# The first feed-forward's output of inner tiles 4 to 15 by seven block products, its modulation rows on GpSimd and ScalarE, and a shorter first look ahead in the second feed-forward

## The chip, the cores and the metric

The kernel runs on one core of a Trainium2 chip. The metric is the device time of one execution in microseconds; lower is better. The time before is the median of three runs.

## What is computed

One layer of a hybrid decoder block, for a sequence of 512 tokens with 1024 features, in float32:

```python
mod = silu(c) @ w_ada + b_ada              # nine rows of 1024: shift, scale, gate for three sub-layers
u = modulate(rmsnorm(h, g1), sh1, sc1)
h = h + 0.5 * gt1 * swiglu(u, w_ffn1_in, w_ffn1_out)
u = modulate(rmsnorm(h, g2), sh2, sc2)
h = h + gt2 * token_mixing(u, ...)         # pooling and dilated attention, gated
u = modulate(rmsnorm(h, g3), sh3, sc3)
h = h + 0.5 * gt3 * swiglu(u, w_ffn2_in, w_ffn2_out)
return rmsnorm(h, g_final)

def swiglu(u, w_in, w_out):
    a, b = split(u @ w_in, 2)              # 1024 -> 2 x 2816
    return (silu(a) * b) @ w_out           # 2816 -> 1024
```

The change touches the two `swiglu` and the computation of `mod`.

## The kernel before

All activations lie transposed, features on partitions, 512 tokens along the free dimension. Each float32 operand is split into a high part (`whi`, `HI`, `UH`) and a remainder (`wlo`, `HK`, `UL`), and each product is three matmuls: high by high, high by low, low by high. ScalarE (ACT) makes the high part with a copy (L312), VectorE (DVE) the low part with a subtraction (L326).

**Tiles and parts.** The 2816 inner features are 22 tiles of 128. `PARTS` groups them as 0 to 3, 4 to 7, 8 to 11, 12 to 15 and 16 to 21. `ffn` walks through the parts: it computes the hidden tiles of a part and one further pair, and then multiplies the hidden tiles of the part by the output weights and adds the result, times the gate, to the residual `H`.

**Two ways to compute hidden tiles.** `ffn_pair` (the first 8 tiles of the first feed-forward, the first 4 of the second) uses plain products, 512 tokens wide. `duo` computes a pair of tiles by seven block products (Strassen's scheme in Winograd's form): the contraction and the tokens are halved, the weights' sums are made on DVE (`make`, L251), the sums of the input once (`u_steps`), and the partial results are moved between PSUM banks and SBUF by ACT (`copy`, L746) and combined by DVE (L788, L807). Each block product is 24 matmuls of 256 tokens (L739 to L741).

**Two ways to compute an output.** The first feed-forward uses the plain one in all parts: 96 matmuls of 512 tokens (L357 to L359), an addition to `H` per output tile (L985). The second uses `out_quad` in its first four parts: seven block products of 24 matmuls with 256 tokens each (L865 to L867), with the hidden tiles' sums from `h_sums`, evictions by ACT (L848), combinations and additions by DVE (L895, L878, L871).

**Order of the weights.** `plan` writes the order in which weights are used. `look(n)` fetches by SyncE's DMA queue and splits weights up to n products ahead into a ring of seven products. For some products of the second feed-forward (`outer`) the low part is made by an ACT copy with scale -1 (L308) and a DMA of GpSimd's queue that accumulates the weights onto it (L310), instead of by DVE. `later(n, f)` puts off a step by n products; `todo` is a list of small steps, popped in the output's loops, such as the trigonometric tables (`trig`) in the third part's output of the first feed-forward.

**Modulation rows.** Each of the 72 columns of `mod` is a row product of 1024 elements, which `ada_do` computes on DVE with one multiplication and its accumulator (L380), from weights fetched by `ada_fetch` (L372). `bg` does one row at a time beside the first feed-forward, with the two buffers `cs` and `AR` from the end of the first part on: twice in each plain pair, and eight times in each plain output of the second to fourth parts, until 48 rows are done.

The engines' instruction order is the order in which this program emits them; each engine works through its own in order.

Of the kernel before, what the change touches and what calls it, by code (L numbers as in the profile page):

```python
# [14 lines left out]
P = 128  # L15
# [3 lines left out]
KT = 8  # L19
# [36 lines left out]
def lay_ffn(w_in, w_out, first, plain, blocks):  # L56

    ins, outs = [], []  # L60
    if first:
        cols = np.concatenate([c for j in range(first) for c in _tiles(j * P, DFF + j * P)])
        for k in range(KT):
            ins.append(w_in[k * P:(k + 1) * P][:, cols])
    for j in range(first, plain):
        for c in _tiles(j * P, DFF + j * P):
            ins.append(_fmajor(w_in, c))
    for j in range(plain, FT, 2):
        for i, c in ((0, 0), (0, DFF), (1, DFF), (1, 0)):
# [12 lines left out]
    outs = [np.concatenate(outs[i:i + 2], axis=1) for i in range(0, n, 2)] + outs[n:]  # L82
    return ins, quads + outs
# [44 lines left out]
NH = 6  # L128
# [15 lines left out]
class Kernel:  # L144
# [6 lines left out]
    def plan(self):  # L151
# [247 lines left out]
    def bg(self):  # L399
# [261 lines left out]
    def ffn_post(self, j, s, pb):  # L661
        nc = self.nc
        h = self.kept[j // 2 % 3][:, j % 2 * T:j % 2 * T + T] if self.kept else self.fw.tile([P, T], F32, name=("hf", "u3")[j % 2])
        nc.vector.tensor_tensor(h, s, pb, op=OP.mult)
        hh, hl = self.HH[j % NH], self.HL[j % NH]
        nc.scalar.activation(hh, h, AF.Copy)
        nc.vector.tensor_tensor(hl, h, hh, op=OP.subtract)

    def ffn_silu(self, j, pa):
        s = self.fw.tile([P, T], F32, name="sl" if j % 2 == 0 else "u2" if not self.kept else "p5")  # L670
        self.nc.scalar.activation(s, pa, AF.Silu)
        return s
# [70 lines left out]
    def duo(self, j, first, last):  # L743
# [15 lines left out]
        p5 = r(self.fw.tile([P, T], F32, name="p5"))  # L759
        if self.kept:  # L760
            c = self.kept[j // 2 % 3]
            u = q(self.fw.tile([P, 2 * T], F32, name="u2"))
            u2, u3 = u[:, :, 0, :], u[:, :, 1, :]
        else:
            c = self.fw.tile([P, 2 * T], F32, name="hf")
            u2, u3 = (r(self.fw.tile([P, T], F32, name=x)) for x in ("u2", "u3"))

        ts = slice(0, 1 if self.kept and j % 4 == 0 and j < PARTS[-1][0] else 2)
# [5 lines left out]
        def high():  # L774
            x = slice(j % NH * T, (j % NH + 2) * T)
            copy(q(self.HHall[:, x])[:, :, ts, :], q(c)[:, :, ts, :])

        def low():
            x = slice(j % NH * T, (j % NH + 2) * T)
            v.tensor_tensor(q(self.HLall[:, x])[:, :, ts, :], q(c)[:, :, ts, :], q(self.HHall[:, x])[:, :, ts, :],  # L780
                            op=OP.subtract)


        for i, (bank, u, start) in enumerate(((A, blk(lo4, T1), True), (B, S[0], True), (A, S[1], False),
                                              (C, blk(hi4, T1), False), (A, S[2], False), (B, S[3], False),
                                              (A, blk(hi4, T2), False))):
            if i == 6:
                v.tensor_tensor(q(c)[:, :, 1, :], p5, u3, op=OP.add)  # L788
            self.look(4)
# [7 lines left out]
            elif i == 1:  # L797
                copy(p5, r(B))
            elif i == 2:
                copy(u2, r(A))  # L800
# [4 lines left out]
            elif i == 6:  # L805
                silu(1, A)
                v.tensor_tensor(q(c)[:, :, 0, :], r(B), u2, op=OP.add)  # L807
# [4 lines left out]
        else:  # L812
            self.later(1, mult)
            self.later(2, high)
            self.later(2, low)

    def h_sums(self, k0):
# [5 lines left out]
        x = slice(k0 % NH * T, (k0 % NH + 2) * T)  # L823
        r = lambda x: x.rearrange("p (j t) -> p j t", j=2)
        to = [(r(h), r(l)) for h, l in self.G] + [(half(self.HHall[:, x], 1), half(self.HLall[:, x], 1))]
# [18 lines left out]
    def out_quad(self, k0, gate):  # L844
# [5 lines left out]
        blk = lambda k, t: [(self.HH[i % NH][:, t], self.HL[i % NH][:, t]) for i in (k, k + 1)]  # L850
# [5 lines left out]
        D = [self.fw.tile([P, 2 * T], F32, name=n).rearrange("p (j h t) -> p j h t", j=2, h=2) for n in ("u2", "sl")]  # L856
        p5 = [r(self.fw.tile([P, T], F32, name=n)) for n in ("p5", "p6")]
# [15 lines left out]
        for i, (bank, u, start) in enumerate(((A, blk(k0, T1), True), (B, G[0], True), (A, G[1], False),  # L873
# [8 lines left out]
            for b in range(2):  # L882
# [11 lines left out]
                elif i == 5:  # L894
                    v.tensor_tensor(D[b][:, :, 0, :], r(B[b]), D[b][:, :, 0, :], op=OP.add)  # L895
        for m in range(4):
# [5 lines left out]
    def ffn2(self):  # L902
        self.put, self.now = [], 0
        self.kept = [self.cond, self.cs, self.AR]
        bk = [self.nb() for _ in range(4)]
        self.head(2, bk, AF.Silu)
        self.G = [(self.tp.tile([P, T], F32R, name="ut"), self.fw.tile([P, T], F32R, name=f"G{i}")) for i in range(3)]
# [11 lines left out]
    def open_ffn(self):  # L919
# [3 lines left out]
        self.HHall, self.HLall = (fp.tile([P, NH * T], F32R, name=x) for x in ("HI", "HK"))  # L923
        self.HH, self.HL = ([x[:, i * T:(i + 1) * T] for i in range(NH)] for x in (self.HHall, self.HLall))
# [17 lines left out]
    def ffn(self, n, j, last=None):  # L942
# [10 lines left out]
        for part, (k0, k1) in enumerate(PARTS):  # L953
            tail = part + 1 == len(PARTS)
            while j < pairs_before(n, part):
# [3 lines left out]
                else:  # L959
                    if self.kept and not tail and j == k1:  # L960
# [7 lines left out]
            hk = [(self.HH[k % NH], self.HL[k % NH]) for k in range(k0, k1)]  # L968
            if not tail and n:
                self.out_quad(k0, gate)  # L970
                continue
            if not tail:
                for m in range(0, KT, 2):
# [8 lines left out]
                    for i, b in enumerate(bs):  # L982
# [4 lines left out]
                        if n == 0 and part:  # L987
                            self.bg()
# [42 lines left out]
    def beside_out(self, part):  # L1031

        if part == 0:
# [5 lines left out]
            self.sums = self.open_sums()  # L1039
            self.todo, last = self.u_steps(0)  # L1040
            return last
        if part == len(PARTS) - 1:
            assert self.ada_next == 48 and not self.adat, self.ada_next
# [423 lines left out]
    def build(self):  # L1467
# [39 lines left out]
        with self.open_ffn():  # L1507
            self.ada_pool = ExitStack()
            self.adaw = self.ada_pool.enter_context(tc.tile_pool(name="f1a", bufs=4))
            self.put, self.now, self.kept = [], 0, None  # L1510
# [4 lines left out]
        with self.open_ffn() as self.f2:  # L1515
# [130 lines left out]
def lay_inputs(x, c, positions, w_ada, b_ada, g_norm_ffn1, w_ffn1_in, w_ffn1_out, g_norm_mix, w_in, w_pool,  # L1646
# [4 lines left out]
    f1i, f1o = lay_ffn(A(w_ffn1_in)[0], A(w_ffn1_out)[0], FIRST, PLAIN[0], False)  # L1651
    f2i, f2o = lay_ffn(A(w_ffn2_in)[0], A(w_ffn2_out)[0], 0, PLAIN[2], True)
# [33 lines left out]
```

## Time and profile before

| | |
|---|---|
| median of 3 runs | 1015.61 us (1015.21 to 1018.82) |
| the profiled execution's own time | 1012.59 us |
| its span | 1010.8 us |
| hidden tiles and outputs of the first feed-forward, from the first duo to the last part's output | 125.9 to 326.9 us |
| the same of the second | 710.4 to 965.8 us |

How the rows of the profile are read: PE is TensorE, PEld its weight loads, DVE VectorE, ACT ScalarE, POOL GpSimd, SP SyncE; a q behind the name is the engine's queue of DMA issues. A row of the view by time gives start, duration (us), engine, line of the kernel, operation, output and inputs with their shapes, a count if several of one kind are merged, and in brackets how long the engine had been idle and what released it. A row of the view by groups gives count, busy time in us, mean ns of one, and the idle time ahead of it. A row of the view by stretches gives its bounds, its length, each engine's busy time, the granted TensorE clock as a share of the full one, the DMA engines' share and GB/s.

### The profile page before, as it was taken

The page shows a single profiled execution, that of the slowest core. Times are in us where ns is not written, and L with a number is a line of the kernel's source. Part 1 is how long each engine was busy: PE and PEld are TensorE (multiplying, and loading weights), DVE is VectorE, ACT ScalarE, POOL GpSimd, SP SyncE. Part 2 cuts the span into 40 slices and gives each one's busy share as a digit, 9 for nine tenths or more (in the row PEclk, how much of TensorE's full clock was granted, in tenths as well). Part 3 has the DMA queues.
Part 4 walks back from the last instruction along what each step waited for, and adds up shares of the span by engine and source line. Part 5 has one row for each costly group of instructions (what it writes and reads, how often), then busy time and mean ns, then how long its engine had stood idle before and what let it go on. Part 6 is the DMA issues. An engine that isn't in the chain of part 4 may idle for free.

```text
span 1010.8 us, 16369 instructions
## 1 busy us (share of the span) xinstructions
PE 996.5 (99%) x6652; PEld 916.6 (91%) x6652; DVE 789.2 (78%) x1182; ACT 496.4 (49%) x754; POOL 47.2 (5%) x54
## 2 busy tenths in 40 slices
PE   8999999999999999999999999999899999999997
PEld 6888898989999899889988888898899999999996
DVE  7978879889786777879447777577998988989754
ACT  6443252625435552233414233463677768677652
POOL 0000000000000000006100000000011011011001
PEclk9999999999999999999999999999999999999998
DMA  8866455555533413122154774321466656756712
GB/s 337 275 217 237 134 201 188 172 165 180 163 110 111 150 40 102 62 84 84 32 182 163 271 260 132 98 74 63 146 147 171 184 147 152 202 128 163 183 32 84
DMA packets 46574, 152.24 MB, mean 151 GB/s; under 512 B 5281, under 2 KB 8609, under 8 KB 46498
## 3 DMA queue, kind: packets, MB, share of 16 engines
q1 hardware_dynamic: 42354, 137.95, 41.0%
q0 software_dynamic: 3456, 12.58, 7.4%
q8 instruction: 52, 0.85, 0.3%
q10 hardware_dynamic: 688, 0.66, 0.2%
q14 instruction: 24, 0.20, 0.1%
HBM read 148.40 MB, written 2.77 MB: 150 GB/s over the span
## 4 chain that ended last, share of the span: by engine, by line
PE 91%; DVE 6%; ACT 1%; issue 1%; DMA 0%; DVEq 0%; ACTq 0%
PE bank L357 14%; PE bank L358 14%; PE bank L359 14%; PE bank L739 10%; PE bank L741 10%; PE bank L740 10%; PE bank L867 3%; PE bank L866 3%; PE bank L865 3%; PE bank L1616 1%; PE bank L1618 1%; PE bank L1620 1%; PE bank L1212 1%; DVE wlo L326 1%; PE bank L1391 1%
## 5 line engine op out<-in xcount | busy, mean ns | idle before, releaser
L326 DVE TENSOR_TENSOR wlo<-raw,whi 128x1024 fp32r<-128x1024 f32 (+7 forms) x161 | 160.1, 1008 | 59.9 <-ACT whi L312 59.5
L312 ACT ACTIVATE whi<-raw 128x1024 fp32r<-128x1024 f32 (+7 forms) x174 | 151.7, 890 | 29.8 <-DVE raw L251 28.1
L357 PE MATMUL bank<-UH,whi 128*128 128x512 f32 (+1 forms) x432 | 158.1, 366 | 0.0
L358 PE MATMUL bank<-UL,whi 128*128 128x512 f32 (+1 forms) x432 | 154.0, 357 | 0.1
L359 PE MATMUL bank<-UH,wlo 128*128 128x512 f32 (+1 forms) x432 | 153.9, 356 | 0.0
L741 PE MATMUL bank<-UH,wlo 128*128 128x256 f32 x512 | 141.8, 277 | 0.0
L739 PE MATMUL bank<-UH,whi 128*128 128x256 f32 x512 | 141.8, 277 | 0.0
L740 PE MATMUL bank<-UL,whi 128*128 128x256 f32 x512 | 141.8, 277 | 0.0
L326 DVE TENSOR_TENSOR wlo<-X,whi 128x1024 fp32r<-128x1024 f32 (+4 forms) x98 | 108.0, 1108 | 27.5 <-ACT whi L312 27.2
L312 ACT ACTIVATE whi<-X 128x1024 fp32r<-128x1024 f32 (+4 forms) x109 | 104.7, 973 | 38.0 <-DVE X L251 37.1
L739 PE MATMUL bank<-SH,whi 128*128 128x256 f32 x384 | 108.0, 281 | 2.9 <-ACT bank L746 2.9
L740 PE MATMUL bank<-SL,whi 128*128 128x256 f32 x384 | 107.6, 280 | 0.0
L741 PE MATMUL bank<-SH,wlo 128*128 128x256 f32 x384 | 107.6, 280 | 0.0
L357 PE MATMUL bank<-HI,whi 128*128 128x512 f32 (+1 forms) x278 | 96.8, 348 | 0.0
L740 PEld LDWEIGHTS bank<-UL,whi 128*128 128x128 f32 x512 | 96.4, 188 | 0.2
L358 PE MATMUL bank<-HK,whi 128*128 128x512 f32 (+1 forms) x278 | 96.5, 347 | 0.0
L739 PEld LDWEIGHTS bank<-UH,whi 128*128 128x128 f32 x512 | 96.2, 188 | 0.2
L359 PE MATMUL bank<-HI,wlo 128*128 128x512 f32 (+1 forms) x278 | 96.4, 347 | 0.0
L741 PEld LDWEIGHTS bank<-UH,wlo 128*128 128x128 f32 x512 | 96.1, 188 | 0.0
L359 PEld LDWEIGHTS bank<-UH,wlo 128*128 128x128 f32 x432 | 81.1, 188 | 12.1
L358 PEld LDWEIGHTS bank<-UL,whi 128*128 128x128 f32 x432 | 81.2, 188 | 11.7 <-issue 0.5
L357 PEld LDWEIGHTS bank<-UH,whi 128*128 128x128 f32 x432 | 81.2, 188 | 11.3 <-issue 0.5
(300 smaller groups left out, 2107.4 us busy)
## 6 DMA issues: line engine op xcount, KB each, us to landing
ada<-wada SPq DMA_DIRECT2D x47, 512.0 KB, 5.0
raw<-wmix SPq DMA_DIRECT2D x44, 512.0 KB, 3.9
raw<-wf1i SPq DMA_DIRECT2D x34, 512.0 KB, 4.6
raw<-wf2i SPq DMA_DIRECT2D x31, 512.0 KB, 3.7
wlo<-wf2i POOLq DMA_DIRECT2D x16, 512.0 KB, 6.2
X<-wf2i SPq DMA_DIRECT2D x13, 512.0 KB, 3.7
cs<-wada SPq DMA_DIRECT2D x12, 512.0 KB, 3.6
AR<-wada SPq DMA_DIRECT2D x12, 512.0 KB, 4.2
```

The lines of the kernel that those rows point to most:

```text
L312: self.nc.scalar.activation(self.hi[:, y], r[:, x], AF.Copy)
L326: self.nc.vector.tensor_tensor(self.lo[:, y], r[:, x], self.hi[:, y], op=OP.subtract)
L357: M(ps, hi, uh, start=start, stop=False)
L358: M(ps, hi, ul, start=False, stop=False)
L359: M(ps, lo, uh, start=False, stop=stop)
L739: M(o, hi, uh, start=start and p == 0 and k == 0, stop=False, skip_group_check=True)
L740: M(o, hi, ul, start=False, stop=False, skip_group_check=True)
L741: M(o, lo, uh, start=False, stop=k == 3, skip_group_check=True)
L865: M(o, hi, uh, start=start and m % 2 == 0 and k == 0, stop=False, skip_group_check=True)
L866: M(o, hi, ul, start=False, stop=False, skip_group_check=True)
L867: M(o, lo, uh, start=False, stop=k == 1, skip_group_check=True)
L1212: M(o, pt[:, blk * P:blk * P + P], v, start=i == 0, stop=i == len(srcs) - 1)
```

## The change

In the first feed-forward, parts two to four use `out_quad` with `h_sums`, so their output weights are laid out in blocks and pass through `blocks` in `plan`. Its duos after the first use the accumulating transfer for two of seven low parts, as those of the second do, and so do its quads. The hidden tiles' high and low parts get four tiles' room instead of six (`nh`), so those of some pairs are put off behind the quad that still reads the old ones. Intermediate tiles (`p5`, `u2`, `hf`) give way to three `kept` tiles. The modulation rows that the plain outputs did on DVE are multiplied by GpSimd and summed by ScalarE's accumulator in `beside`, after the second, fourth and sixth product of each duo and quad; the rows in plain pairs stay on DVE. The trigonometric steps are popped one per quad product. In the second feed-forward, the first duo's first product looks 3 products ahead instead of 4.

```diff
@@ lay_ffn
-        if blocks and k1 < FT:
+        if blocks <= k0 and k1 < FT:
@@ plan
-                        blocks(ins[at:at + 4], n == 2 and j > PLAIN[n])
+                        blocks(ins[at:at + 4], j > PLAIN[n])
...
-                put = blocks if n and part < len(PARTS) - 1 else plain
+                put = blocks if (n or part) and part < len(PARTS) - 1 else plain
@@ bg
         self.ada_do(self.ada_next)
+        self.bg_next()
+
+    def bg_next(self):
         self.ada_next += 1
         self.bg_fetch()
...
+    def bg_end(self):
+
+        if self.pending is None:
+            return
+        j, t = self.pending
+        self.pending = None
+        self.nc.scalar.activation(t, t, AF.Copy, accum_out=self.mod[:, j:j + 1])
+        self.ada_free.append(t)
+        self.bg_next()
+
+    def beside(self, i):
+
+        if self.nh != 4 or i not in (1, 3, 5) or self.ada_next >= self.ada_stop:
+            return
+        self.bg_end()
+        if self.ada_next < self.ada_stop and self.ada_next in self.adat:
+            t = self.adat.pop(self.ada_next)
+            self.nc.gpsimd.tensor_tensor(t, t, self.cond, op=OP.mult)
+            self.pending = self.ada_next, t
@@ ffn_post
+        if self.nh == 4 and j in (4, 5):
+            t = slice(0, HT)
+            self.later(5, lambda: nc.scalar.activation(hh[:, t], h[:, t], AF.Copy))
+            self.later(5, lambda: nc.vector.tensor_tensor(hl[:, t], h[:, t], hh[:, t], op=OP.subtract))
+            return
@@ duo
-            self.look(4)
+            self.look(3 if self.nh != 4 and first and i == 0 else 4)
...
+            self.beside(i)
...
-            self.later(2, high)
-            self.later(2, low)
+            n = 8 if self.nh == 4 and j % 4 == 0 else 2
+            self.later(n, high)
+            self.later(n, low)
@@ out_quad
+            if self.nh == 4 and self.todo:
+                self.todo.pop(0)()
+            self.beside(i)
@@ ffn
-                    if self.kept and not tail and j == k1:
+                    if not tail and j == k1:
                         self.h_sums(k0)
...
-            if not tail and n:
+            if not tail and (n or part):
                 self.out_quad(k0, gate)
                 continue
...
-                        if n == 0 and part:
-                            self.bg()
@@ beside_out
+            self.open_G()
...
+            self.bg_end()
@@ build
-        with self.open_ffn():
+        with self.open_ffn(4):
...
-        with self.open_ffn() as self.f2:
+        with self.open_ffn(6) as self.f2:
@@ lay_inputs
-    f1i, f1o = lay_ffn(A(w_ffn1_in)[0], A(w_ffn1_out)[0], FIRST, PLAIN[0], False)
+    f1i, f1o = lay_ffn(A(w_ffn1_in)[0], A(w_ffn1_out)[0], FIRST, PLAIN[0], PARTS[1][0])
```

More of the change, by code (lines that the diff above doesn't have):

```diff
@@ L82, in lay_ffn @@
     outs = [np.concatenate(outs[i:i + 2], axis=1) for i in range(0, n, 2)] + outs[n:]
-    return ins, quads + outs
+    return ins, outs[:-KT] + quads + outs[-KT:]
 def qk_cols(base, g, second):
@@ L758, in duo @@
         r = lambda x: x.rearrange("p (j t) -> p j t", j=2)
[L759 to L768, printed above, removed]
+        u3 = r(self.fw.tile([P, T], F32, name="u3"))
+        c = self.kept[j // 2 % 3]
+        c0, c1 = q(c)[:, :, 0, :], q(c)[:, :, 1, :]
+        ts = slice(0, 1 if j % 4 == 0 and j < PARTS[-1][0] else 2)
+        HHp, HLp = (q(x) for x in self.hpair(j))
         silu = lambda h, bank: nc.scalar.activation(q(s)[:, :, h, :], r(bank), AF.Silu)
@@ L822, in h_sums @@
         h11, h21, h12, h22 = half(a, 0), half(a, 1), half(b, 0), half(b, 1)
-        x = slice(k0 % NH * T, (k0 % NH + 2) * T)
         r = lambda x: x.rearrange("p (j t) -> p j t", j=2)
-        to = [(r(h), r(l)) for h, l in self.G] + [(half(self.HHall[:, x], 1), half(self.HLall[:, x], 1))]
+        to = [(r(h), r(l)) for h, l in self.G] + [tuple(half(x, 1) for x in self.hpair(k0))]
         def add(o, x, y, op):
@@ L855, in out_quad @@
         r = lambda x: x.rearrange("p (j t) -> p j t", j=2)
-        D = [self.fw.tile([P, 2 * T], F32, name=n).rearrange("p (j h t) -> p j h t", j=2, h=2) for n in ("u2", "sl")]
-        p5 = [r(self.fw.tile([P, T], F32, name=n)) for n in ("p5", "p6")]
+        D = [self.kept[k // 2 % 3].rearrange("p (j h t) -> p j h t", j=2, h=2) for k in (k0, k0 + 2)]
+        p5 = self.fw.tile([P, 2 * T], F32, name="sl")
+        p5 = [r(p5[:, i * T:(i + 1) * T]) for i in range(2)]
         def product(banks, u, start):
@@ L967, in ffn @@
             nk = k1 - k0
-            hk = [(self.HH[k % NH], self.HL[k % NH]) for k in range(k0, k1)]
-            if not tail and n:
+            hk = [self.hh(k) for k in range(k0, k1)]
+            if not tail and (n or part):
                 self.out_quad(k0, gate)
@@ L1506, in build @@
         self.ada_free, self.ada_depth = None, 3
-        with self.open_ffn():
+        with self.open_ffn(4):
             self.ada_pool = ExitStack()
             self.adaw = self.ada_pool.enter_context(tc.tile_pool(name="f1a", bufs=4))
-            self.put, self.now, self.kept = [], 0, None
+            self.put, self.now = [], 0
             self.startup()
```

50 lines of the change are left out of this document (29 added, 21 removed).

## The prediction, made before the result was known

> **What bounds the kernel now.** I read the page first, then the busy time of each engine stage by stage, then the order in time of the stages that the change touches.
>
> ```profile
> span 1010.8 us, 16369 instructions
> PE 996.5 (99%) x6652; PEld 916.6 (91%) x6652; DVE 789.2 (78%) x1182; ACT 496.4 (49%) x754; POOL 47.2 (5%) x54
> ```
>
> TensorE (PE) is the bound, but a share over the whole span says little of one stage. The stretches below are: a plain output of the first feed-forward; its two duos (a duo is one pair of inner tiles by seven block products) at tiles 10 to 13 of the next part; then in the second feed-forward the first duo, the first quad (one part's output by seven block products), a whole round of two duos and a quad, the quad of that round alone, two duos, and two later quads.
>
> ```profile
> core 0: us, PE busy (x) PEld busy (x) DVE busy (x) ACT busy (x) POOL busy (x), PEclk, DMA share, GB/s
> 145.20:167.00 21.80, 21.80 (x98) 18.06 (x97) 18.67 (x25) 5.57 (x6) 0.00 (x0) 1.00 0.52 162
> 227.30:266.60 39.30, 39.25 (x337) 39.02 (x336) 34.72 (x41) 21.13 (x28) 0.00 (x0) 1.00 0.59 183
> 710.40:734.70 24.30, 21.41 (x169) 21.17 (x168) 23.27 (x27) 16.94 (x24) 0.00 (x0) 0.93 0.42 149
> 734.70:754.50 19.80, 19.80 (x171) 19.80 (x170) 18.08 (x23) 14.89 (x21) 2.75 (x3) 1.00 0.67 165
> 754.50:812.00 57.50, 57.50 (x506) 57.50 (x505) 50.92 (x63) 41.39 (x56) 5.21 (x6) 1.00 0.64 164
> 793.00:812.00 19.00, 19.00 (x170) 19.00 (x169) 17.27 (x23) 14.52 (x21) 2.43 (x3) 1.00 0.66 168
> 812.00:850.50 38.50, 38.50 (x339) 38.50 (x339) 34.05 (x41) 26.93 (x36) 2.80 (x4) 1.00 0.63 164
> 850.50:869.90 19.40, 19.40 (x171) 19.30 (x170) 17.68 (x23) 14.45 (x21) 2.40 (x3) 1.00 0.69 168
> 908.40:927.40 19.00, 19.00 (x170) 19.00 (x169) 17.38 (x22) 14.91 (x21) 2.47 (x3) 1.00 0.65 166
> ```
>
> The second feed-forward already does in every round what the first is to do, so its rounds are the model. In them PE has no gap, and VectorE (DVE) is busy 50.92 of 57.5 us: only 6.6 us are left. That is the number on which the rest hangs.
>
> **Part by part. 1, the quads.** Three plain outputs of 21.8 us become quads of 19.0, 19.4 and 19.0: 65.4 - 57.4 = 8.0 us saved on PE. The pair of duos at 227.30 took 39.3 where a pair takes 38.5 (57.5 - 19.0, and 812.00 to 850.50); the multiplications of modulation rows ahead of it leave DVE, so I count that 0.8 too. **8.8 us saved.** The duos of the first feed-forward now also take two of seven low halves by a GpSimd accumulating transfer instead of DVE; pairs with and without it take 38.5, so PE gains nothing.
>
> **2, the sums of the hidden tiles** come into the first duo, which had none. The first duo of the second feed-forward, which has them, shows the load: DVE 23.27 of 24.30 us, then 18.08 of 19.80.
>
> ```profile
> 126.10 0.69 DVE L664 TENSOR_TENSOR u<-u,bank 128x512 f32<-128x512 f32 x1 [1.49 <-PE bank L359]
> 714.25 0.68 DVE L664 TENSOR_TENSOR cs<-p,bank 128x512 f32<-128x512 f32 x1
> 754.54 1.22 DVE L251 TENSOR_TENSOR raw<-X,raw 128x1024 f32<-128x1024 f32 x1
> ```
>
> From the product of the last plain pair (L664) to the end of the quad's work DVE's queue takes 754.54 - 714.25 = 40.3 us. Set at 126.10 it ends at 166.4; PE alone would end duo and quad at 125.9 + 19.3 + 19.1 = 164.3. **2.1 us late.** Bounds: 0 if the look ahead covers it, and 5.7, by which the model's own duo and quad (24.3 + 19.8) pass 38.4; its wait and clock, in part 4, make most of that, so I stay near the row of DVE.
>
> **3, the modulation rows.** Twenty rows (ten in each of cs and AR) leave DVE, and GpSimd (POOL) multiplies them.
>
> ```profile
> L380 DVE SCALAR_TENSOR_TENSOR cs<-cs,cond 128x1024 f32<-128x1024 f32 x10 | 12.2, 1218 | 0.0
> L1177 ACT ACTIVATION_READ_ACCUMULATOR prob<-prob,negmax 128x1 f32 x32 | 6.0, 187 | 0.0
> L312 ACT ACTIVATE whi<-raw 128x1024 fp32r<-128x1024 f32 x107 | 112.0, 1050 | 10.3 <-DVE raw L251 8.6 <-DMA raw<-wmix 1.3 <-DMA raw<-wf1i 0.4
> L1272 POOL TENSOR_TENSOR rt<-rt 128x527 f32<-128x527 f32 x2 | 2.1, 1064 | 2.9 <-DVE wlo L326 2.3 <-ACT rt L1266 0.6
> ```
>
> DVE is rid of 1.22 us a row. ScalarE (ACT) gains 1.05 + 0.19 = 1.24; nine in a round make 41.4 + 11.2 = 52.6 of 57.5, off the path, though the evictions of PE's banks stand in the queue behind each. The next row's fetch now waits on SP's queue for ACT instead of DVE, with weight loads behind it; ACT is the less loaded of the two, so I count nothing for that. The splits of the hidden tiles that are put off by five or eight products are as many as before and keep their order; nothing again, unless DVE is late already, and then they are in its sum. POOL pays 1064 x 1024 / 527 = 2.07 us a row, 41 us in all. No row shows that multiplication itself, or what it does to DVE in this stage; the nearest rows are in the mixing stage and the tail:
>
> ```profile
> 471.47 3.07 POOL L1272 TENSOR_TENSOR rt<-rt 128x527 f32<-128x527 f32 x2 [0.61 <-ACT rt L1266]
> 474.62 1.92 POOL L1272 TENSOR_TENSOR rt<-rt 128x521 f32<-128x521 f32 x1
> 472.30 1.31 DVE L326 TENSOR_TENSOR wlo<-raw,whi 128x1024 fp32r<-128x1024 f32 x1 [1.13 <-ACT whi L312]
> 474.22 1.40 DVE L326 TENSOR_TENSOR wlo<-raw,whi 128x1024 fp32r<-128x1024 f32 x1 [0.60 <-ACT whi L312]
> 484.56 1.23 DVE L326 TENSOR_TENSOR wlo<-raw,whi 128x1024 fp32r<-128x1024 f32 x1 [1.65 <-ACT whi L312]
> 996.40 2.32 POOL L565 TENSOR_TENSOR out<-out,AR 128x256 f32<-128x256 f32 x3
> 994.70 0.42 DVE L596 TENSOR_TENSOR AR<-AR,ut 128x256 f32<-128x256 f32 x1 [0.54 <-ACT ut L510]
> 997.24 0.88 DVE L596 TENSOR_TENSOR AR<-AR,ut 128x256 f32<-128x256 f32 x1 [0.55 <-ACT ut L510]
> ```
>
> At 471.47 the first of two 1.06 us operations ends at 472.53; DVE's low half began at 472.30 and takes 1.31 instead of 1.23. POOL's second ends at 474.54, 2.0 us later instead of 1.06: it stood while DVE ran. The next low half began at 474.22, under POOL, and ends at 475.62, one bare run after 474.54; POOL's third took 1.92, again standing. In the tail 0.42 becomes 0.88 beside POOL. The two engines take turns, a whole instruction at a time, where both read two operands from SBUF. The Trainium skill says so too (SBUF — State Buffer, Who interferes with whom): a VectorE instruction with two SBUF inputs and a GpSimd instruction that reads SBUF lock the shared port for the whole instruction; these rows agree, 1.40 against 1.23 us.
>
> Not all of DVE's work is of that sort. In a round the PSUM readers are:
>
> ```profile
> 747.08 1.65 DVE L871 SCALAR_TENSOR_TENSOR H<-bank,mod,H 128x256 f32<-128x256 f32 x4
> 752.14 0.68 DVE L895 TENSOR_TENSOR u<-bank,u 128x512 f32<-128x512 f32 x1
> 736.91 0.69 DVE L807 TENSOR_TENSOR AR<-bank,u 128x512 f32<-128x512 f32 x1
> ```
>
> twice each, 6.0 us; (50.9 - 6.0) / 57.5 = 0.78 of the time DVE works on two SBUF operands. So a row on POOL holds DVE for b = 0.78 x 2.07 = 1.6 us; ends 0 (all in gaps) and 2.07. Three multiplications start in each duo and quad: six in the first duo and quad, nine in the next round, five in the two duos after (the twentieth row starts there). What each can hide:
>
> - first duo and quad: 2.1 + 6b late;
> - round: 9b - 6.6 + 2.0 (seven small trigonometric steps, moved from the plain output, at most 0.29 each by the row below);
> - two duos: 5b - (38.5 - 34.05) = 5b - 4.45.
>
> ```profile
> L1072 DVE SCALAR_TENSOR_TENSOR tr<-tr 128x128 f32<-128x128 f32 x4 | 1.2, 292 | 0.0
> ```
>
> Together 20b - 7.0 = 25.0. The quad and duos behind carry no rows, and the splits run four products ahead; I estimate 2 us of the last lag never reaches PE. **23 us lost.** The Trainium skill gives 4497 ns for 2048 elements (GPSIMD Engine Reference, Elementwise — side-by-side cycle accounting); half is an estimate of 2.25 us a row, and the loss by it 26; no run here shows that length.
>
> **4, the shorter first look** in the second feed-forward. PE's one long wait there:
>
> ```profile
> 715.51 1.04 ACT L312 ACTIVATE whi<-raw 128x1024 fp32r<-128x1024 f32 x1
> 718.55 0.58 ACT L746 ACTIVATE bank<-bank 128x512 f32<-128x512 f32 x1
> 719.18 0.58 PE L739 MATMUL bank<-SH,whi 128*128 128x256 f32 x1 [2.89 <-ACT bank L746]
> 724.81 0.58 ACT L746 ACTIVATE u<-bank 128x512 f32<-128x512 f32 x1
> 726.22 0.28 PE L739 MATMUL bank<-SH,whi 128*128 128x256 f32 x1
> ```
>
> And the stretch after the wait, where PE has thirteen matmuls at a granted clock of 0.51:
>
> ```profile
> 719.20:722.10 2.90, 2.90 (x13) 2.90 (x14) 2.57 (x4) 2.33 (x3) 0.00 (x0) 0.51 0.38 112
> ```
>
> With the look at three the eviction follows the split of 715.51 directly and ends near 717.05, so PE starts some 2.1 us sooner. But the product at 726.22 needs the eviction of 724.81, which hangs on DVE's queue; that queue loses one idle half microsecond, so 724.9 is the earliest: 1.3 us gained. Bounds: 0, and 4.3 (the wait, and 1.4: 2.9 us for what takes 13 x 2.72 / 24 = 1.5, a product of 24 matmuls being 19.0 / 7 = 2.72).
>
> The sum: -8.8 + 23 - 1.3 = **+12.9**. The profiled execution took 1012.59 us (span 1010.8, 1.8 around it), 3.0 below the median of 1015.61; the profile becomes 1025.5 and the median, which I predict, 1028.5.
>
> **Rivals.** *The multiplications slip in beside DVE* (faster): the two delays of 472.30 and 474.22 were 0.08 and 0.17 us. If b stays near there, only the 2.1 of the first duo remains: -8.8 + 2.1 - 1.3 = -8.0, 1007.6. The point of change is b = 0.96 us, where 20b - 9 equals the 10.1 gained. Against it: both delays were short because DVE began late under a running POOL operation, and DVE had idled before.
>
> *The accumulating transfers stand behind the multiplications* in POOL's queue, DVE being free:
>
> ```profile
> 752.21 0.86 POOL L310 DMA_DIRECT2D wlo<-wf2i  x1 [10.91 <-ACT wlo L308]
> ```
>
> ```profile
> wlo<-wf2i POOLq DMA_DIRECT2D x16, 512.0 KB, 6.2
> AR<-wada SPq DMA_DIRECT2D x12, 512.0 KB, 4.2
> ```
>
> Landed at 758.4, used by the fourth product at 754.5 + 3 x 2.75 = 762.7: 4.3 us to spare. A row fetched in 4.2 and multiplied in 2 to 3 can hold it up by as much; a half microsecond in seven duos and quads makes 3.5: 1011.1. The quad's own eviction order speaks for it, POOL's many idle microseconds against.
>
> *The clock*: if half of the twenty waits also bring a granted clock of 0.51 as at 719.20, 1.4 us each: 1042.5. A wait of 2.9 us brought it; the ones expected are near 1.6.
>
> **Chances.** Forecast 0.67 (its own range, b from 1.2 to 2.07: 1020.6 to 1038.0), multiplications beside DVE 0.17, queue 0.10, clock 0.06. From 1007 to 1038 leaves out the clock and the lower half of the first rival. A measurement of this kernel tells about 0.5%, 5.1 us, from no change. Slower by more: 0.62 of the forecast (b over 1.2) and 0.06, 0.68. Faster: 0.17 and 0.03 of the queue, 0.20. The rest, 0.12.
>
> **What would show it.** Right: PE idle in the first feed-forward between 126 and about 290, released by ACT evictions that wait on DVE; L326 and L251 there well over 1.22 us beside POOL; POOL multiplications of 2 to 3.2 us, twenty; quads of 19 us only where no rows run (the third). The first duo of the second feed-forward some 1.3 us shorter. Wrong: mean L326 at 1.23 beside POOL and PE without gaps: then the first rival; transfers landing late at the fourth product: the second.

## The result

The changed kernel takes 1044.89 us (median of four runs, 1042.85 to 1047.56), the kernel before in the same job 1015.41: a ratio of 1.030, 95% interval 1.0278 to 1.0322. It is 29.5 us slower, where 12.9 slower was forecast; 1044.9 lies above the range of 1007 to 1038. The profiled execution took 1044.7 us. Its page begins so:

```profile
span 1042.9 us, 16997 instructions
PE 1001.9 (96%) x6868; PEld 928.5 (89%) x6868; DVE 828.2 (79%) x1193; ACT 559.5 (54%) x857; POOL 120.9 (12%) x92
```

The spans differ by 32.1 us, but PE's busy time by only 5.4: the rest is new idle time. The busy time by stage shows where. The rows are the first duo, the first quad, two duos, the second quad, two duos, the third quad, two duos:

```profile
core 0: us, PE busy (x) PEld busy (x) DVE busy (x) ACT busy (x) POOL busy (x), PEclk, DMA share, GB/s
125.60:147.70 22.10, 19.76 (x170) 19.51 (x169) 21.10 (x24) 15.08 (x23) 5.04 (x3) 1.00 0.56 188
147.70:170.90 23.20, 20.59 (x170) 20.39 (x169) 21.51 (x21) 18.60 (x29) 14.98 (x6) 0.93 0.69 205
170.90:220.20 49.30, 42.77 (x339) 41.77 (x338) 48.46 (x41) 30.26 (x46) 20.67 (x11) 0.93 0.71 192
220.20:243.80 23.60, 20.17 (x170) 19.44 (x169) 20.96 (x28) 18.61 (x28) 8.51 (x5) 1.00 0.71 204
243.80:294.60 50.80, 42.98 (x338) 41.99 (x337) 49.96 (x48) 32.80 (x49) 18.08 (x10) 0.93 0.65 176
294.60:314.70 20.10, 19.33 (x170) 19.13 (x169) 18.64 (x28) 17.26 (x27) 2.61 (x3) 1.00 0.65 167
314.70:353.60 38.90, 38.90 (x339) 38.88 (x338) 29.78 (x36) 23.86 (x32) 2.59 (x3) 1.00 0.70 168
```

In the five stages that carry rows VectorE is busy 93 to 98% of the time in four and 89% in the other; it is the bound there, and PE stands 2.3 to 7.8 us in each. The two duos take 49.3 and 50.8 us instead of 38.5. Where no rows are left, in the third quad and behind it, the lengths come near those of the prediction (20.1 where 19.0 was expected, 38.9 where 38.5). The busy time over the whole stretch, kernel before first, then after:

```profile
125.90:326.92 201.02, 200.97 (x1465) 189.48 (x1464) 168.89 (x203) 92.64 (x122) 0.00 (x0) 1.00 0.50 161
```

```profile
125.59:353.56 227.97, 204.47 (x1682) 201.08 (x1680) 210.41 (x218) 156.46 (x229) 72.49 (x38) 0.96 0.67 184
```

The stretch grows by 26.95 us. Of the rest of the 32.1, 2.8 lie between its end and the second feed-forward, 2.5 in the second feed-forward, and 0.3 go the other way at the start.

VectorE's own groups, 125 to 295 us, say why it is late; each of these instructions took 1.22 us before, as in the first row, which is the kernel before's (126 to 327 us):

```profile
L326 DVE TENSOR_TENSOR wlo<-X,whi 128x1024 fp32r<-128x1024 f32 x30 | 36.7, 1223 | 7.9 <-ACT whi L312 7.8
```

```profile
L325 DVE TENSOR_TENSOR wlo<-X,whi 128x1024 fp32r<-128x1024 f32 x19 | 30.8, 1620 | 3.3 <-ACT whi L311 3.3
L250 DVE TENSOR_TENSOR X<-raw,X 128x1024 f32<-128x1024 f32 x10 | 21.5, 2147 | 0.0
L250 DVE TENSOR_TENSOR X<-X 128x1024 f32<-128x1024 f32 x9 | 15.8, 1761 | 0.0
```

PE's waits in the stretch are those that the prediction named (L778, evictions by ScalarE), with a smaller one in the quads, on an accumulating transfer. The prediction's second rival named that one; it is 4.8 us here and 2.2 without rows (run 1 below), so of what the rows cost it can be 2.6 at most:

```profile
PE bank L778 <- ACT kept L785: 10.5, 5, 3.1
PE bank L778 <- ACT bank L785: 5.8, 4, 3.2
PE bank L900 <- DMA wlo<-wf1o: 4.8, 3, 2.6
```

Ahead of those evictions in its queue ScalarE waits for VectorE; no wait of its own for GpSimd is on record in this stretch:

```profile
ACT whi L311 <- DVE X L250: 30.2, 16, 4.5
```

**How the two engines share.** GpSimd's instructions at the first quad, then VectorE's:

```profile
146.96 6.52 POOL L434 TENSOR_TENSOR cs<-cs,cond 128x1024 f32<-128x1024 f32 x1 [15.68 <-DMA cs<-wada]
153.42 2.02 POOL L309 DMA_DIRECT2D wlo<-wf1o  x2
155.13 2.78 POOL L434 TENSOR_TENSOR AR<-AR,cond 128x1024 f32<-128x1024 f32 x1
```

```profile
149.99 1.22 DVE L250 TENSOR_TENSOR X<-X 128x1024 f32<-128x1024 f32 x1
151.13 0.68 DVE L838 TENSOR_TENSOR kept<-bank,kept 128x512 f32<-128x512 f32 x1
152.34 2.21 DVE L325 TENSOR_TENSOR wlo<-X,whi 128x1024 fp32r<-128x1024 f32 x1 [0.53 <-ACT whi L311]
154.48 1.21 DVE L806 TENSOR_TENSOR kept<-sl,kept 128x1024 f32<-128x1024 f32 x1
155.62 3.38 DVE L250 TENSOR_TENSOR X<-raw,X 128x1024 f32<-128x1024 f32 x1
```

GpSimd's row of 146.96 makes no headway while VectorE goes from one instruction with two SBUF operands to the next. At 151.13 VectorE reads a bank of PSUM; the row ends 2.35 us after that, a row's bare length (2.40, below). VectorE's next instruction, of 152.34, ends 1.1 after the row: it stood until then. The row of 155.13 ends at 157.91, and the instruction of 155.62 at 159.00, 1.1 later. So a waiting instruction gets nothing until the other engine's instruction is over. At 146.96 five of VectorE's instructions, begun after GpSimd's, also got ahead of it. That row is the exception: the other nineteen take 2.40 to 3.41 us, so they wait 1.0 us at most. One of them, and VectorE's instruction beside it:

```profile
211.72 2.74 POOL L434 TENSOR_TENSOR cs<-cs,cond 128x1024 f32<-128x1024 f32 x1 [5.95 <-DMA cs<-wada]
```

```profile
210.98 1.22 DVE L250 TENSOR_TENSOR X<-raw,X 128x1024 f32<-128x1024 f32 x1
212.11 3.43 DVE L325 TENSOR_TENSOR wlo<-X,whi 128x1024 fp32r<-128x1024 f32 x1
```

This row got in as soon as the instruction of 210.98 had ended, and the one of 212.11 stood until the row was over at 214.46. Both queues were full here too; why the row of 146.96 was passed over and this one was not, no run shows.

### The profile page after: what moved, and what is told of

Same layout as the page of the kernel before. It is cut to its first block, busy times and chain, and to the rows that moved or that the text cites. A ratio compares the mean times of both kernels' runs of the same rounds, so it can differ in the third digit from the quotient of the medians.

```text
span 1042.9 us, 16997 instructions
## 1 busy us (share of the span) xinstructions
PE 1001.9 (96%) x6868; PEld 928.5 (89%) x6868; DVE 828.2 (79%) x1193; ACT 559.5 (54%) x857; POOL 120.9 (12%) x92
## 4 chain that ended last, share of the span: by engine, by line
PE 74%; DVE 15%; DMA 4%; issue 4%; ACT 2%; SPq 0%; DVEq 0%; ACTq 0%
PE bank L356 12%; PE bank L357 12%; PE bank L358 12%; PE bank L778 6%; PE bank L780 6%; PE bank L779 6%; DVE wlo L325 5%; PE bank L900 3%; PE bank L898 3%; PE bank L899 3%; DVE X L250 2%; DMA wlo<-wf2i 2%; PE bank L1656 1%; PE bank L1660 1%; PE bank L1658 1%
## 5 line engine op out<-in xcount | busy, mean ns | idle before, releaser
L325 DVE TENSOR_TENSOR wlo<-raw,whi 128x1024 fp32r<-128x1024 f32 (+5 forms) x132 | 147.3, 1126 | 51.7 <-ACT whi L311 51.5
L311 ACT ACTIVATE whi<-raw 128x1024 fp32r<-128x1024 f32 (+5 forms) x157 | 149.1, 961 | 28.5 <-DVE raw L250 17.9
L325 DVE TENSOR_TENSOR wlo<-X,whi 128x1024 fp32r<-128x1024 f32 (+3 forms) x118 | 122.6, 1061 | 27.5 <-ACT whi L311 27.3
L311 ACT ACTIVATE whi<-X 128x1024 fp32r<-128x1024 f32 (+3 forms) x135 | 117.0, 886 | 47.3 <-DVE X L250 47.2
L778 PE MATMUL bank<-UH,whi 128*128 128x256 f32 x512 | 141.9, 277 | 0.4 <-ACT u L785 0.3
L778 PE MATMUL bank<-SH,whi 128*128 128x256 f32 x384 | 111.8, 291 | 19.4 <-ACT kept L785 10.5
L779 PE MATMUL bank<-SL,whi 128*128 128x256 f32 x384 | 110.5, 288 | 0.0
L780 PE MATMUL bank<-SH,wlo 128*128 128x256 f32 x384 | 110.5, 288 | 0.0
L778 PEld LDWEIGHTS bank<-UH,whi 128*128 128x128 f32 x512 | 96.2, 188 | 0.9 <-ACT u L785 0.8
L778 PEld LDWEIGHTS bank<-SH,whi 128*128 128x128 f32 x384 | 76.0, 198 | 21.6 <-ACT kept L785 11.5
L357 PEld LDWEIGHTS bank<-UL,whi 128*128 128x128 f32 x432 | 81.2, 188 | 11.8 <-issue 0.5
L780 PEld LDWEIGHTS bank<-SH,wlo 128*128 128x128 f32 x384 | 76.1, 198 | 0.0
L779 PEld LDWEIGHTS bank<-SL,whi 128*128 128x128 f32 x384 | 76.1, 198 | 0.0
```

What stands on the lines that cost most here:

```text
L311: self.nc.scalar.activation(self.hi[:, y], r[:, x], AF.Copy)
L325: self.nc.vector.tensor_tensor(self.lo[:, y], r[:, x], self.hi[:, y], op=OP.subtract)
L357: M(ps, hi, ul, start=False, stop=False)
L778: M(o, hi, uh, start=start and p == 0 and k == 0, stop=False, skip_group_check=True)
L779: M(o, hi, ul, start=False, stop=False, skip_group_check=True)
L780: M(o, lo, uh, start=False, stop=k == 3, skip_group_check=True)
```

## The experiments

The theory was the prediction's own: a multiplication on GpSimd holds VectorE. The rivals: the quads alone are slow; ScalarE's sums or the order in the queues cost the time; the clock. The profiled executions begin the first duo between 125.2 and 128.8 us, according to when the clock first rose (11 to 20 us), so stages are counted from the first duo on. "The stretch" is that from there to the end of the last duo, as above; VectorE's busy time in it is from the same row.

**1. No rows** (left out of the computation: the multiplication and the sum of the twenty rows; their columns are zero, the weights are still fetched).

```
 beside():
-    t = self.adat.pop(self.ada_next)
-    self.nc.gpsimd.tensor_tensor(t, t, self.cond, op=OP.mult)
-    self.pending = self.ada_next, t
+    self.ada_free.append(self.adat.pop(self.ada_next))
+    self.bg_next()
```

> The changed kernel with the twenty modulation rows left out of the duos and quads: neither multiplied nor summed, their weights still fetched. Port theory (GpSimd's multiplications hold VectorE's two-operand work): the loss goes with them, 1003 to 1011 us. Theory that the quads and their sums overload VectorE by themselves: most of the loss stays, above 1030. ScalarE theory (the sums delay the evictions): 1003 to 1011 as well, told apart by the memset run.

1011.58 us, ratio to before 0.9975 (0.9961 to 0.9989).

```profile
125.45:322.20 196.75, 193.99 (x1681) 193.14 (x1680) 171.00 (x218) 137.20 (x189) 15.78 (x18) 1.00 0.75 213
```

The stretch is 4.3 us shorter than before, and the rows are worth 31.2 of it (227.97 - 196.75). They also raise VectorE's busy time from 171.00 to 210.41 us with the same 218 instructions: 39.4 us, **1.97 us held by each row**. The quads gain less than forecast: PE waits twice in them for an accumulating transfer:

```profile
PE bank L899 <- DMA wlo<-wf1o: 2.2, 2, 1.5
```

**2. The rows on VectorE**, at the same places.

```
 beside():
-    self.bg_end()
-    ... (multiplication by GpSimd)
+    self.bg()
```

> The changed kernel with the twenty rows done on VectorE at the same places, 1.31 us each, GpSimd and ScalarE free of them. Port theory: VectorE's lag by the prediction's formula with b = 1.31 is 20 x 1.31 - 9 = 17, so about 1015.4 - 10 + 17 = 1022, range 1014 to 1030, clearly below the 1044.9 of the change. Theory that ScalarE's sums or GpSimd's queue are to blame: 1003 to 1012.

1027.55 us, ratio 1.0124 (1.0101 to 1.0148), 17 us faster than the changed kernel. The stretch is 208.51, VectorE's busy time 193.61: 1.13 us a row instead of 1.97. Moving a row off VectorE made it cost VectorE more.

**3. Memsets in place of the multiplications** (the rows are overwritten by zeros, so the modulation is another one; the sums stay).

```
-    self.nc.gpsimd.tensor_tensor(t, t, self.cond, op=OP.mult)
+    for _ in range(2):
+        self.nc.gpsimd.memset(t, 0.0)
```

> The changed kernel with each multiplication replaced by two memsets of the same tile on GpSimd, so that it writes but reads nothing from SBUF; the sums on ScalarE stay (the rows are left out of the result). Port theory: VectorE runs its two-operand instructions at 1.22 us beside them and the time is 1003 to 1014. ScalarE theory: nothing changes, above 1035. Queue theory (accumulating transfers behind long GpSimd work): the loss shrinks only as the memsets are shorter than 3 us.

1013.2 us, ratio 0.9994 (0.9979 to 1.0009). GpSimd works some 39 us on the memsets (20 of each buffer, 1.0 us each), ScalarE has its sums, and VectorE is as fast as alone (171.01 us busy in the stretch, 171.00 in run 1); the groups of GpSimd and of VectorE:

```profile
L435 POOL MEMSET AR<- 128x1024 f32 x20 | 20.2, 1008 | 26.5 <-DMA AR<-wada 23.9 <-ACT whi L311 2.1
```

```profile
L325 DVE TENSOR_TENSOR wlo<-X,whi 128x1024 fp32r<-128x1024 f32 x25 | 30.5, 1222 | 9.4 <-ACT whi L311 9.4
```

So neither GpSimd's writing, nor the releases, nor the sums by themselves cost anything to speak of: what holds VectorE is that GpSimd reads SBUF. The Trainium skill (SBUF — State Buffer, Who interferes with whom) says just this: a VectorE instruction with two SBUF inputs contends with a GpSimd instruction that reads SBUF, not with one that only writes it, and the other side blocks for the whole instruction. Runs 1 and 3 agree: 1.97 us held by a row that reads, none by a memset. In that section the engine that issues first gets the port; here GpSimd's row of 146.96 stood behind instructions that VectorE started after it, while the other nineteen agree.

**4. A quarter and 5. a half of each row** (only the first 256 or 512 columns are multiplied; the sums take all of the row).

```
-    self.nc.gpsimd.tensor_tensor(t, t, self.cond, op=OP.mult)
+    self.nc.gpsimd.tensor_tensor(t[:, :W], t[:, :W], self.cond[:, :W], op=OP.mult)   # W = 256, 512
```

> The changed kernel, but GpSimd multiplies only the first 256 of the 1024 columns of each row; the row is still fetched whole, and ScalarE still sums all of it (the modulation so made is another one). As many instructions, waits and releases as before, each multiplication a quarter as long, 0.6 to 0.75 us instead of 2.4 to 3.1. If the time that a multiplication holds VectorE is what costs: 20 x some 2.3 us saved of some 3.0, so the lag of a round, 9 x 0.7 less the slack of 4.6 us, is 1 to 2 us, and no wait is long enough to bring the half clock: 1013 to 1020 us. If the cost is one of count and order (the extra instruction and its waits in GpSimd's and ScalarE's queues): still over 1035.

> The changed kernel with GpSimd multiplying the first 512 of the 1024 columns of each row (the sum still takes all of it, so the modulation is another one). A row alone takes 0.73 us at a quarter and 2.40 us whole, so about 1.29 here. If the loss is the time that VectorE is held less the free time it has: 0.78 x 1.29 = 1.0 us a row, 20 x 1.0 - 9 = 11 over the kernel without rows at 1011.6: 1020 to 1027 us. If a multiplication costs by being started at all (VectorE's running chain keeps GpSimd out, and ScalarE's sum waits for it): near the quarter, 1016 to 1020. If the loss is in proportion to the columns: half of 33, 1028 or more.

1017.84 us, ratio 1.0038 (1.0022 to 1.0054), and 1023.66, ratio 1.0104 (1.0069 to 1.0138). With as many instructions and waits as in the changed kernel the loss goes from 33.3 us over the kernel without rows to 6.3 and 12.1. Half the width costs about a third, though its four runs spread from 1019.9 to 1028.6 us. That the first part of the hold falls into VectorE's free time would explain it. But a quarter costs more than the hold explains (VectorE's busy time in the stretch is 176.52, so 5.5 us in all, which the free time of a round holds). Its longest wait of PE, read back from PE to ScalarE, GpSimd and VectorE, shows a second way to lose:

```profile
213.11 0.58 PE L898 MATMUL bank<-ut,whi 128*128 128x256 f32 x1 [2.77 <-ACT sl L803]
```

```profile
209.53 1.06 ACT L423 ACTIVATE cs<-cs 128x1024 f32<-128x1024 f32 x1 [4.05 <-POOL cs L434]
...
212.48 0.57 ACT L803 ACTIVATE sl<-bank 128x512 f32<-128x512 f32 x1
```

```profile
201.60 7.90 POOL L434 TENSOR_TENSOR cs<-cs,cond 128x256 f32<-128x256 f32 x1 [8.49 <-DMA cs<-wada]
209.47 0.73 POOL L434 TENSOR_TENSOR AR<-AR,cond 128x256 f32<-128x256 f32 x1
```

```profile
208.82 0.68 DVE L838 TENSOR_TENSOR kept<-bank,kept 128x512 f32<-128x512 f32 x1
```

A multiplication of 0.73 us took 7.90: it stood while VectorE went through two-operand instructions from 201.6 to its next PSUM reader at 208.82. ScalarE's sum stood 4.05 us for it, and the eviction that PE needed stood behind the sum. This happened twice in the twenty rows (5.71 and 7.90 us); the other eighteen took 0.73 to 2.73. In the half-width run six of twenty took 3.5 to 8.7 us, where 1.29 is the bare length.

**6. No sums** (ScalarE's sums left out, the columns zero; the multiplications whole).

```
 bg_end():
-    self.nc.scalar.activation(t, t, AF.Copy, accum_out=self.mod[:, j:j + 1])
```

> The changed kernel with GpSimd's multiplications whole, but ScalarE's sums of the rows left out (their twenty modulation columns are set to zero). If the multiplications hold VectorE and VectorE is late by itself: 1038 to 1045 us, the sums' 1.24 us a row lying beside other work of ScalarE. If instead a sum that waits for a late multiplication is what keeps the evictions of PE's banks waiting in ScalarE's queue: under 1030, although sums behind short memsets cost nothing.

1040.96 us, ratio 1.0266 (1.0241 to 1.0291). The sums are worth 3.9 us when VectorE is late; in run 3, where it is not, sums and memsets together are worth 1.6 (1013.2 - 1011.58), which is not clear of the noise. The multiplications alone make most of the loss.

**7. The rows alone**, with plain outputs, and three rows in each of seven duos.

```
-    if not tail and (n or part):
+    if not tail and n:
         self.out_quad(k0, gate)
 ... (weights, halves and sums of hidden tiles likewise as for plain outputs)
```

> The rows' part of the change without the quads: in the first feed-forward all outputs are plain ones of 21.8 us again, without sums of hidden tiles; the rows are multiplied by GpSimd and summed by ScalarE three to a duo, seven duos, and none beside the outputs, where VectorE then idles some 10 us. Buffers and accumulating transfers as in the changed kernel. If a multiplication holds VectorE for its own length wherever it runs: a pair of duos needs 33.6 + 6 x 2.2 = 46.8 us of VectorE in 38.5, less some 4 that the look ahead hides, so some 4 lost in each of three pairs and 1 to 3 in the first duo, and the half clock up to five times 1.7: 1025 to 1037 us. If the loss needs the quads, VectorE having no time to catch up anywhere: the plain outputs absorb it, 1013 to 1019.

1017.86 us, ratio 1.0038 (1.0019 to 1.0057).

```profile
128.69:334.40 205.71, 202.25 (x1465) 189.76 (x1464) 165.37 (x151) 125.70 (x178) 63.13 (x34) 1.00 0.64 187
```

This run goes by the second of the two expectations. Rows alone lengthen the stretch by 4.7 us, quads alone shorten it by 4.3, and both together lengthen it by 26.95. VectorE's instructions are stretched here too (L250 `X<-raw,X` 1764 ns on average), but pairs of duos take 39.7 instead of 49.3 and 50.8: in the plain outputs, with no rows and less of its own work, VectorE catches up. The loss is in the combination, since the quads take away the free time on which the rows' hold would have landed.

**8. Each row in four pieces.**

```
+    for i in range(4):
+        x = slice(i * HT, i * HT + HT)
+        self.nc.gpsimd.tensor_tensor(t[:, x], t[:, x], self.cond[:, x], op=OP.mult)
```

> The changed kernel with each row multiplied by GpSimd in four instructions of 256 columns instead of one of 1024; nothing else is changed. Alone the four take 4 x 0.73 = 2.9 us instead of 2.40. If an instruction holds the port as a whole and hands it over at its end, VectorE gets in between the pieces, so a single VectorE instruction waits at most 0.7 us, but the sum that VectorE is held grows with the 2.9: 1042 to 1056 us. If what matters is the longest wait, since the look ahead of four products covers short ones: 1020 to 1035.

1043.76 us, ratio 1.0295 (1.0278 to 1.0312): no remedy. VectorE's busy time in the stretch is 208.95, a hold of 1.90 us a row. By this it is the sum of the holds that counts, not the length of one. PE's waits are divided in another way, though: 9.8 us of them are on accumulating transfers, which GpSimd issues in the same queue, instead of 4.8.

**9. The shorter look alone**, on the kernel before, **and 10. the changed kernel without it.**

```
-    self.look(4)
+    self.look(3 if self.kept and first and i == 0 else 4)     # 9; the reverse in 10
```

> The kernel before with the shorter first look ahead in the second feed-forward alone. By the prediction: 1.3 us faster, 1014. By the trace of the changed kernel, whose first duo there took 24.86 instead of 24.28 us with two waits and the granted clock halved again: no change, 1014.5 to 1016.5.

> The changed kernel with the first look of the second feed-forward at four products again. By the prediction's step for it, 1.3 us slower than the changed kernel: 1046. By the run of that edit alone (its first duo 1.2 shorter, its first quad 1.4 longer): no difference, 1044 to 1045.5, with the first duo of the second feed-forward 24.3 us or more and the quad behind it under 20.

1012.94 us, ratio 0.9991 (0.9977 to 1.0004), and 1044.39, ratio 1.0299 (1.027 to 1.0329) where the changed kernel had 1.030: the look is worth nothing that can be measured. Run 9's first duo and first quad of the second feed-forward, and PE's waits there:

```profile
711.10:734.20 23.10, 20.17 (x170) 19.57 (x169) 22.00 (x26) 15.60 (x23) 0.00 (x0) 1.00 0.43 155
734.20:755.30 21.10, 19.47 (x170) 19.28 (x169) 19.31 (x26) 15.85 (x23) 2.75 (x3) 1.00 0.65 155
```

```profile
PE bank L739 <- ACT u L746: 2.2, 1, 2.2
PE bank L867 <- DMA wlo<-wf2o: 1.6, 1, 1.6
PE bank L739 <- ACT bank L746: 0.7, 1, 0.7
```

The one wait of 2.9 us has become two, of 0.7 and 2.2. PE stands as long as before in the duo (23.10 - 20.17 us, where the kernel before has 24.30 - 21.41), so the 1.2 us that the duo gains are not the wait's but the clock's, which was not halved here. The same duo in the changed kernel (short look), then in run 10 (long look):

```profile
739.90:764.70 24.80, 21.66 (x169) 21.26 (x168) 24.10 (x29) 18.01 (x25) 0.58 (x1) 0.93 0.42 147
```

```profile
743.10:766.50 23.40, 19.83 (x170) 19.43 (x169) 22.46 (x26) 16.27 (x24) 0.00 (x0) 1.00 0.47 155
```

With the short look it is the longer one, against the prediction, and the expectation of run 10 (24.3 us or more, with a quad under 20) missed: 23.4, and a quad of 20.4. In all thirteen profiled executions the duo takes 24.3 to 24.9 us where the clock was halved in it (six) and 23.0 to 23.4 where it was not (seven), with either look. What a shorter duo gains, the quad behind it mostly gives back (21.1 instead of 19.8 us in run 9): PE comes there sooner, and waits for the accumulating transfer, which the kernel before met already landed. Duo and quad together take 43.0 to 44.7.

**11. One quad**, meant as a faster version: only the third output by block products, all rows on VectorE, eight beside each plain output and one in each of four duos.

```
-    put = blocks if (n or part) and part < len(PARTS) - 1 else plain
+    put = blocks if (n or part > 2) and part < len(PARTS) - 1 else plain
 beside():
+    if self.nh == 4 and i == 3:
+        self.bg()
 ... (bg() again beside the plain outputs; weights, halves and sums likewise)
```

> A version for speed: only the third output in question (hidden tiles 12 to 15) by seven block products; the rows stay on VectorE, eight beside each of the two outputs before it, which stay plain, and one in each of the duos at tiles 8, 10, 12 and 14. By the stage lengths 21.8 - 19.4 = 2.4 us saved, VectorE holding 17.0 + 1.3 us a duo of 19.25: 1010.5 to 1013 where the kernel before takes 1013.8. If one row a duo already makes VectorE late, or the accumulating transfers do: 1014 to 1017.

1017.4 us, ratio 1.0037 (1.0024 to 1.0049): slower than before, and the expectation missed. The quad takes 19.04 us as hoped, 2.74 less, but the duos with a row each take 19.87, 39.34 and 41.00 instead of 19.33, 38.53 and 39.28; the stretch is 201.2, as before. So the stretch does not hold the 3.4 us by which the median is longer. In the profiled execution 0.9 us more lie in the mixing stage, 0.6 in the second feed-forward, and 2.9 ahead of the first duo, where the clock rose later; what the median's 3.4 us are was not found. No version tried here is measurably faster than the kernel before and complete.

## Why the prediction was wrong in size

- **Part 3, the hold: the step that failed first.** "POOL pays 1064 x 1024 / 527 = 2.07 us a row" scaled the mean of two operations of another shape (527 columns each). A row that VectorE leaves alone takes 2.40 us (that of 124.30, ahead of the first duo), and the hold is 1.97 us instead of 1.6. The share of 0.78 was nearly right: 0.78 x 2.40 = 1.87. With 1.97 the formula gives 20 x 1.97 - 7.0 - 2 = 30.4 us instead of 23, and that is 7.4 of the 19.2 us by which the spans' 32.1 passes the forecast 12.9. By the estimate of 2.25 us a row, half of the Trainium skill's 4497 ns for 2048 elements (GPSIMD Engine Reference, Elementwise — side-by-side cycle accounting), the loss would have been 26 instead of 23; the measured 2.40 is nearer to that estimate than to mine.

```profile
124.30 2.40 POOL L434 TENSOR_TENSOR cs<-cs,cond 128x1024 f32<-128x1024 f32 x1 [123.86 <-DVE AR L379]
```

- **The size of the hold alone does not take the time out of the range:** 1.97 lies within the prediction's own bounds for it (1.2 to 2.07), and 12.9 + 7.4 would have made 1035.9. The other 11.8 us are 2.4 in parts 1 and 2, 2.9 that the rows cost beyond the formula, 1.3 in part 4 that did not come, and 5.2 outside the stretch.
- **Part 3, the formula of the lag.** Of its 30.4 us, 2.1 are the first duo's own (part 2), so it gives 28.3 for the rows; measured are 31.2 (the stretch with and without rows). For the rows on VectorE (1.13 us each) it gives 11.5, and 11.8 were lost. It fails for short holds: 3.8 for the half row (a hold of 0.74, with VectorE busy 185.87 us), where 9.6 were lost, and nothing for the quarter, where 5.8 were. It has no term for sums and evictions that stand behind a late multiplication in ScalarE's queue (run 4), nor for the transfers.
- **Part 3, "take turns"** was right for nineteen of twenty rows: a row waits out VectorE's instruction, and VectorE's next one waits out the row. One row of 6.52 us (and one of 7.90 among the quarter rows) was passed over by a run of VectorE's instructions. "Off the path" for ScalarE's sums was wrong, by 3.9 us (run 6).
- **Parts 1 and 2** were forecast at -8.8 + 2.1 = -6.7; without rows the stretch is 4.3 shorter, so 2.4 us too much was hoped for. First duo and first quad take 41.9 us there instead of 38.4, so part 2 is 3.5 and not 2.1. The model rounds of the second feed-forward had no wait on an accumulating transfer in a quad; here there are some (2.2 us in run 1, 4.8 in the changed kernel).
- **The clock** was priced as a rival by itself, at half of twenty waits. It came along with the forecast instead, five times in the stretch. One of them:

```profile
178.70:182.10 3.40, 3.40 (x18) 3.40 (x18) 3.40 (x4) 1.59 (x2) 2.40 (x2) 0.50 0.63 177
```

  At the granted clock of 0.50 such a spell costs PE up to 1.7 us, together up to 8.5, and the rows do raise PE's busy time in the stretch by 10.5 us (193.99 to 204.47). But VectorE was late in these stages anyway: in run 2, where the mean clock was 0.99, it is busy for the same share of the stretch (93%) as in the changed kernel (92%). That speaks for a small part of the clock in the loss; how much it is was not settled.
- **Part 4** gained 0 instead of 1.3: the step "that queue loses one idle half microsecond, so 724.9 is the earliest" ended with the second wait. In the changed kernel the clock was halved behind that wait, and the duo takes 24.8 us instead of 24.3; in run 9 it was not, and the quad's wait for a transfer took back what the duo gained.
- **Put at nothing and not foreseen:** 2.8 us between the end of the stretch and the second feed-forward, and 2.5 in it instead of a gain. Two waits in the mixing stage are new:

```profile
PE bank L356 <- DVE H L1500: 0.9, 1, 0.9
PE bank L358 <- DVE wlo L325: 0.5, 1, 0.5
```

  Runs 1 to 6, 8 and 10, which have the changed kernel's buffers and quads, show the same two gaps; in run 7, with the buffers but plain outputs, they are gone, and in run 11 one of them is. What makes them was not tried.
- **Right:** the place of the loss, its engine and its carrier; VectorE's instructions well over 1.22 us, the row lengths (eighteen of twenty between 2 and 3.2 us), the third quad near 19 (20.1), and that it is slower. The rival that the multiplications slip in beside VectorE, with its point of change at a hold of 0.96 us, falls at 1.97.

## What to carry to other kernels

Before work is moved from VectorE to GpSimd, look at the operands of VectorE's own instructions in that stage: where most read two from SBUF, a GpSimd instruction that reads SBUF costs VectorE most of its own length, here 1.97 of 2.40 us, for work that took VectorE 1.13. Then compare the sum of these holds with the free time of the same round, not of the kernel, because two edits that each cost or gain 4 us alone can cost 27 together when one of them uses up the free time that the other needs. An operation of a new shape is scaled from a row of the same shape or bounded generously; a wait that goes is followed through the next stage, too.

## What was unexpected of the hardware

- GpSimd can be kept out for long, one row in twenty in the changed kernel: a multiplication of 0.73 us took 7.90, and one of 2.40 took 6.52, each until VectorE read PSUM. Most rows were let in after one instruction of VectorE.
- GpSimd's memset of the same tile (1.01 us on average) left VectorE at 1222 ns.
- The clock was halved for 3.4 us after PE's standing of as little as 1.77 us (the gap that ends at 178.42), but not after one of 2.34 (at 139.38). The Trainium skill (TensorE: Matmul & The Clock Gate, Part 1) tells of a free-running window of about 3.4 us. The traces agree: the five spells in the stretch begin at 158.25, 178.73, 209.45, 253.82 and 284.54 us, which are 6, 9, 13 and 9 steps of 3.41 us apart. Counted on that grid, a gap matters by how much of it falls into one window. The gap that ends at 178.42 lies whole in one window; the one of 2.34 is cut in two by an edge at 137.77 and leaves 1.61 in the second window. In the changed kernel up to the end of the second feed-forward, half clock followed each window in which PE stood 1.77 us or more, and none in which it stood 1.61 or less; over all thirteen traces, from full clock, the two groups overlap between 1.77 and 1.86.
